# Latent adaLN sums in blocks of 128 rows by 1024 columns, with one sum tile, in a diffusion block on one Trainium2 core

## The chip, the cores and the metric

The kernel runs on one core of one Trainium2 chip. The metric is the device time of one execution in microseconds. Before the change the median of three runs is 1408.22 us (1406.82 to 1408.33). A profiled execution, from which all rows come, took 1407.89 us, of which the trace spans 1406.1 us from the first instruction to the last.

## What is computed

One layer of a diffusion backbone over 256 latent tokens x and 256 context tokens ctx, both 2048 wide, in fp32: neighbourhood attention with 16 heads, then a gated feed-forward part, each with a shift, a scale and a gate from a condition vector (adaLN). Cut to what matters:

```python
sh1, sc1, g1, sh2, sc2, g2 = adaln(cond_lat, w_ada, b_ada)   # silu(c) @ w_ada + b, six parts of 2048
h  = modulate(rms_norm(x, norm_mix_g), sh1, sc1)
hc = modulate(rms_norm(ctx, norm_mix_g), csh1, csc1)
y, _ = neighbourhood_attention(h, hc, w_qkv, q_g, k_g, rpb, w_o, False)
x  = x + g1 * y
hf = modulate(rms_norm(x, norm_ffn_g), sh2, sc2)
x  = x + g2 * conv_ffn(hf, w_up, conv_w, conv_b, w_down)
```

The change concerns the four parts g1, sc2, sh2 and g2 for the latent tokens: four products of one vector of 2048 with a matrix of 2048 x 2048.

## The kernel before

**Products.** All large products are made on TensorE (PE) in three parts: each weight tile of two blocks of 128 rows by up to 512 columns (a pair) is loaded by SP's queue into wr (four buffers), cast by ScalarE (ACT) into a high half wh (L166) and subtracted by VectorE (DVE) into a low half wl (L170). Two pairs are split ahead of use, and wl has two buffers, so pair n can be split when PE is done with pair n-2. PE then needs wh and wl. The stages: an opening with the norms and the first adaLN parts (to about 205 us); then, head group by head group, projections of q (two tiles of rows) and k and v (four tiles) over the 2048 columns of w_qkv, 512 columns at a time; the products with w_o; those with w_up; those with w_down.

**Attention** is cut into steps (scores, softmax, turn, weighted sum) that a list `side` hands out, some after every tile of a projection (`tick`). The turn transposes the softmax rows pr on PE into a bank ms, and ACT and DVE split the result into pth (L648) and ptl (L649). The weighted sum (L658, L661, L662) needs both, and its result is split by ACT (L578) and DVE (L579) into om, which the w_o products read. Heads 0 to 11 are done before the last v projection ends; their results wait in oT, and L579 also splits these. The last four heads run beside and behind the last v projection, up to the middle of the w_o products. The v tiles are split into vv (L572).

**The latent adaLN parts** are not products on PE. For one column group of 512 outputs, DVE multiplies each block of weight rows by the condition (one number per partition) and adds it into a tile acc (L289 for the first, L291 for the rest; 16 instructions for 2048 rows). Then PE transposes acc by four blocks of 128 into a bank ms (L299), and DVE reduces this (L302), adds the bias (L305) and, for the scale, the gain (L307). A second list `ada` hands these pieces out: a piece is a load of 512 KB into wa and two sums. Twelve column groups (g1, the scale gs2, the shift sh2) run between 220 and 665 us, with ADA_RATE pieces per tile of a projection (0.5 at four tiles, 0.1 at two) and 0.6 per pair in the w_o products; what is left is drained before the last w_o group. Four more, for g2, run in the w_up stage with two buffers. The loads run three pieces ahead. acc has two buffers, and a group's end (transposes, reduction) is called with the second piece of the next.

**What sets the order.** The program is written in the order in which the pieces are called, and a scheduler then puts each engine's instructions in one fixed row from its own estimate of durations, by priority and by when operands and buffers are free. Each engine works its row off in order; an instruction that waits holds all behind it. The banks ms (two buffers) serve adaLN transposes, scores, turns and weighted sums.

Of the kernel before, what the change touches and what calls it, by code (L numbers as in the profile page):

```python
# [9 lines left out]
F32 = mybir.dt.float32  # L10
F32R = mybir.dt.float32r
AF = mybir.ActivationFunctionType
ALU = mybir.AluOpType
AX = mybir.AxisListType

P = 128
D = 2048
T = 256
KD = D // P
# [6 lines left out]
CH = 512  # L26
KT = 2

RATE, RATE3 = 0.46, 0.36

ADA_RATE = {2: 0.1, 4: 0.5}

WA = 4

# [5 lines left out]
S_C, S_GM, S_GF, S_B, S_QG, S_KG = 0, 32, 48, 64, 160, 161  # L40
# [15 lines left out]
def block_kernel(  # L56
# [13 lines left out]
    nc = tc.nc  # L70
    cp = ctx.enter_context(tc.tile_pool(name="cp", bufs=1))
    wp = ctx.enter_context(tc.tile_pool(name="wp", bufs=1))
# [7 lines left out]
    def ms():  # L80
        return ps.tile([P, CH], F32, tag="ms", name="ms", bufs=2)
# [12 lines left out]
    sm = cp.tile([P, S_END], F32, name="sm")  # L94
    nc.sync.dma_start(sm, small)
    ident = cp.tile([P, P], F32, name="ident")
# [8 lines left out]
    for half in range(2):  # L105
# [3 lines left out]
            out=lo, in_=lo, pattern=[[1, GRID - WIN]], compare_op=ALU.is_ge, fill=NEG,  # L109
# [4 lines left out]
            out=hi, in_=hi, pattern=[[-1, GRID - WIN]], compare_op=ALU.is_ge, fill=NEG,  # L114
            base=WIN // 2 - 1 - WIN, channel_multiplier=1,
        )
    sT = cp.tile([P, KD, 2], F32, name="sT")
# [9 lines left out]
    g1T = cp.tile([P, KD], F32, name="g1T")  # L127
    sh2T = cp.tile([P, KD], F32, name="sh2T")
    gs2T = cp.tile([P, KD], F32, name="gs2T")
    g2T = cp.tile([P, KD], F32, name="g2T")  # L130
# [4 lines left out]
    nc.scalar.dma_start(rp, rpb)  # L135


    def wload(src, k0, kn, c0, cn, pool=None, bufs=WA):

        if pool:  # L140
            w = pool.tile([P, KT, CH], F32, tag="wa", name="wa", bufs=bufs)
        else:
            w = wp.tile([P, KT, CH], F32, tag="wr", name="wr", bufs=4)
        nc.sync.dma_start(
            w[:, :kn, :cn],
            src[k0 * P : (k0 + kn) * P, c0 : c0 + cn].rearrange("(k p) f -> p k f", p=P),
        )
        return w
# [122 lines left out]
    def ada_tasks(pool, i, c, dst, gcol=None, bufs=WA):  # L271

        st = {}

        def load(q):
            st[q] = wload(w_ada, q * KT, KT, i * D + c * CH, CH, pool, bufs)

        def part(q):
            w = st[q]
            if q == 0:
                st["acc"] = pool.tile([P, CH], F32, tag="acc", name="acc", bufs=2)
            acc = st["acc"]
            for k in range(KT):
                s = sT[:, q * KT + k, 0:1]
                if q == 0 and k == 0:
                    nc.vector.tensor_scalar_mul(acc, w[:, k, :], s)  # L289
                else:  # L290
                    nc.vector.scalar_tensor_tensor(  # L291
                        out=acc, in0=w[:, k, :], scalar=s, in1=acc, op0=ALU.mult, op1=ALU.add
                    )

        def finish():
            acc = st["acc"]
            sp = ms()
            for b in range(4):
                nc.tensor.transpose(sp[:, b * P : (b + 1) * P], acc[:, b * P : (b + 1) * P], ident)  # L299
            d = dst[:, 4 * c : 4 * c + 4]  # L300
            bc = S_B + i * KD + 4 * c
            nc.vector.tensor_reduce(  # L302
                out=d, in_=sp.rearrange("p (b t) -> p b t", t=P), axis=AX.X, op=ALU.add
            )
            nc.vector.tensor_add(d, d, sm[:, bc : bc + 4])  # L305
            if gcol is not None:
                nc.vector.scalar_tensor_tensor(  # L307
                    out=d, in0=d, scalar=1.0, in1=sm[:, gcol + 4 * c : gcol + 4 * c + 4],
                    op0=ALU.add, op1=ALU.mult,
                )  # L310

        return [(lambda q=q: load(q), lambda q=q: part(q)) for q in range(KD // KT)], finish

    def ada_pieces(cols, bufs=WA):

        loads = [l for pairs, _ in cols for l, _ in pairs]
        parts = [p for pairs, _ in cols for _, p in pairs]
        n = KD // KT

        def piece(i):  # L320
            if i == 0:
                for load in loads[: bufs - 1]:
                    load()
            if i + bufs - 1 < len(loads):
                loads[i + bufs - 1]()
            if i % n == 1 and i > n:
                cols[i // n - 1][1]()
            with tc.issue_after(last[0]), tc.issue_after(last[1]):
                if i < len(parts):
                    parts[i]()  # L330
                else:
                    cols[-1][1]()

        return [lambda i=i: piece(i) for i in range(len(parts) + 1)]


    hp = ctx.enter_context(tc.tile_pool(name="hp", bufs=1))
# [68 lines left out]
    loads = []  # L406
# [116 lines left out]
    ap = actx.enter_context(tc.tile_pool(name="ap", bufs=1))  # L523
# [154 lines left out]
            return [seq, w[0] + s[2] + t[2] + w[1] + s[3] + w[2] + t[3] + w[3]]  # L678
        return [seq + w[0] + s[2] + w[1] + t[2] + s[3] + w[2] + t[3] + w[3]]

    cols = [ada_tasks(ap, 2, c, g1T) for c in range(4)]
    cols += [ada_tasks(ap, 4, c, gs2T, S_GF) for c in range(4)]
    cols += [ada_tasks(ap, 3, c, sh2T) for c in range(4)]
    ada.extend(ada_pieces(cols))

    v, v1 = [[split_v([vsums[g][:, tt, :] for tt in range(4)], g)] for g in range(2)]
# [10 lines left out]
    k = split_k(out_of_psum(kps, kw))  # L697
    q = split_q(out_of_psum(project(0, 2), qw))
    for g in range(3):
        side.extend(sum(attention(g, q, k, v), []))  # L700
        c0 = (g + 1) * CH
# [238 lines left out]
        side.tick(1.6)  # L940
        ada.tick(0.25)

    later = ada_pieces([ada_tasks(fp, 5, c, g2T, bufs=2) for c in range(4)], 2)
    hfv = lambda kt, c: hf[:, kt, c]
    xgv = lambda kt, c: xg(kt, int(c.start > 0))
    for c0 in range(0, FF, CH):
# [82 lines left out]
```

## Time and profile before

| | |
|---|---|
| median of three runs | 1408.22 us (1406.82 to 1408.33) |
| profiled execution | 1407.89 us, span 1406.1 us |
| PE busy | 1380.3 us, 98% |
| DVE busy | 1028.0 us, 73% |
| ACT busy | 703.0 us, 50% |
| DMA moved | 317 MB, mean 226 GB/s |
| mean granted TensorE clock | 0.999 |

Busy time of PE is near to the whole span. Where PE is idle for a moment, the views name what it waited for: a tile, the engine and the line that wrote it last. A time such as 573.99 is counted from the first instruction of the span. Two instructions of an engine may overlap by a tenth of a microsecond in the rows, so what one costs its engine is read from start to start.

### The profile page before, as it was taken

To read this page: it belongs to the slowest core of one execution; us is meant where nothing else is said; L and a number is where in the kernel's file an instruction comes from. 1 tells how busy PE (TensorE), PEld (TensorE's weight loads), DVE (VectorE), ACT (ScalarE), POOL (GpSimd) and SP (SyncE) were. 2 spreads that over 40 slices of the span, in tenths; PEclk is the share of its full clock that TensorE was granted. 3 is DMA by queue.
4 is the path that set the end of the run, shared out by engine and by line. 5 is a ranking of instruction groups with operands and counts; after the bars stand their busy time and mean duration, and the time that the engine had idled before them with its cause. 6 is when DMAs were issued, how large, how long until landed. Compare 5 with 4: busy or idle time off the path is not lost.

```text
span 1406.1 us, 20819 instructions
## 1 busy us (share of the span) xinstructions
PE 1380.3 (98%) x7672; PEld 1167.7 (83%) x7672; DVE 1028.0 (73%) x1694; ACT 703.0 (50%) x1218; POOL 57.1 (4%) x57
## 2 busy tenths in 40 slices
PE   4999999999999999999999999999999999999999
PEld 2565778888888888888988888888888888888888
DVE  4555678879877979789898887878878675545454
ACT  4322254564444573554676565656556564333333
POOL 1000010121010121000000000000000000000000
PEclk9999999999999999999999999999999999999999
DMA  9998737767775868666767777777776666566554
GB/s 306 357 352 285 234 98 236 230 216 253 228 245 184 278 204 281 193 206 208 239 187 251 241 227 233 233 239 236 241 233 204 179 189 208 184 207 203 171 178 145
DMA packets 208919, 317.14 MB, mean 226 GB/s; under 512 B 23360, under 2 KB 87744, under 8 KB 208816
## 3 DMA queue, kind: packets, MB, share of 16 engines
q1 hardware_dynamic: 208688, 315.79, 71.7%
q8 instruction: 60, 0.98, 0.3%
q14 instruction: 43, 0.35, 0.1%
q10 hardware_dynamic: 128, 0.01, 0.0%
HBM read 312.75 MB, written 3.01 MB: 225 GB/s over the span
## 4 chain that ended last, share of the span: by engine, by line
PE 95%; DVE 2%; DMA 1%; SPq 1%; ACT 0%; issue 0%; DVEq 0%; ACTq 0%
PE pj L745 20%; PE pj L752 11%; PE mx L745 9%; PE pj L390 8%; PE pj L389 8%; PE pj L391 8%; PE ms L745 8%; PE mx L752 5%; PE ms L752 4%; PE mx L389 2%; PE ms L424 2%; PE mx L390 2%; PE mx L391 2%; PE ms L644 1%; SPq L418 1%; DMA xc<-in_ctxT 1%
## 5 line engine op out<-in xcount | busy, mean ns | idle before, releaser
L170 DVE TENSOR_TENSOR wl<-wr,wh 128x1024 fp32r<-128x1024 f32 (+2 forms) x425 | 478.6, 1127 | 253.1 <-ACT wh L166 127.2
L166 ACT CAST wh<-wr 128x1024 fp32r<-128x1024 f32 (+2 forms) x425 | 414.2, 976 | 485.2 <-PE pj L745 117.6
L390 PE MATMUL pj<-wl,hh 128*128 128x512 f32 x512 | 203.1, 397 | 0.0
L391 PE MATMUL pj<-wh,hl 128*128 128x512 f32 x512 | 200.0, 393 | 0.0
L389 PE MATMUL pj<-wh,hh 128*128 128x512 f32 x512 | 193.7, 397 | 2.5 <-ACT hh L463 2.5
L291 DVE SCALAR_TENSOR_TENSOR acc<-wa,sT,acc 128x512 f32<-128x512 f32 x240 | 185.0, 773 | 1.9
L745 PE MATMUL pj<-hf,wh 128*128 128x512 f32 x624 | 146.3, 391 | 0.0
L745 PEld LDWEIGHTS pj<-hf,wh 128*128 128x128 f32 x624 | 115.6, 188 | 23.0
L389 PEld LDWEIGHTS pj<-wh,hh 128*128 128x128 f32 x512 | 96.0, 189 | 26.6 <-issue 3.4
L390 PEld LDWEIGHTS pj<-wl,hh 128*128 128x128 f32 x512 | 96.8, 189 | 21.6 <-DVE wl L170 0.9
L391 PEld LDWEIGHTS pj<-wh,hl 128*128 128x128 f32 x512 | 96.5, 189 | 18.8
L745 PE MATMUL mx<-hf,wh 128*128 128x512 f32 x352 | 94.6, 390 | 0.0
L745 PE MATMUL ms<-hf,wh 128*128 128x512 f32 x336 | 90.5, 389 | 0.0
L752 PEld LDWEIGHTS pj<-hf,wl 128*128 128x128 f32 x624 | 77.5, 192 | 1.6
L752 PE MATMUL pj<-hf,wl 128*128 128x256 f32 x624 | 78.0, 283 | 0.0
L745 PEld LDWEIGHTS mx<-hf,wh 128*128 128x128 f32 x352 | 64.7, 188 | 12.3
L745 PEld LDWEIGHTS ms<-hf,wh 128*128 128x128 f32 x336 | 63.1, 188 | 13.3
L491 DVE TENSOR_TENSOR vsum<-vsum,mx 128x512 f32<-128x512 f32 x64 | 43.2, 684 | 34.2 <-PE mx L391 34.0
L897 ACT ACTIVATE y<-z,sm 128x256 f32<-128x256 f32 x86 | 51.8, 603 | 11.6 <-DVE z L880 10.0
L389 PE MATMUL mx<-wh,hh 128*128 128x512 f32 x128 | 52.7, 412 | 0.2
L424 PE MATMUL ms<-wx,s 128*32 128x512 f32 (+1 forms) x288 | 37.2, 587 | 15.4 <-DMA wx<-in_w_ada 15.4
L390 PE MATMUL mx<-wl,hh 128*128 128x512 f32 x128 | 50.7, 396 | 0.0
(264 smaller groups left out, 2036.8 us busy)
## 6 DMA issues: line engine op xcount, KB each, us to landing
wr<-in_w_up SPq DMA_DIRECT2D x160, 512.0 KB, 4.4
wa<-in_w_ada SPq DMA_DIRECT2D x128, 512.0 KB, 5.0
wr<-in_w_qkv SPq DMA_DIRECT2D x93, 512.0 KB, 4.2
wr<-in_w_down SPq DMA_DIRECT2D x63, 512.0 KB, 4.7
wx<-in_w_ada SPq DMA_DIRECT2D x56, 512.0 KB, 8.7
wr<-in_w_o SPq DMA_DIRECT2D x24, 512.0 KB, 5.0
wr<-in_w_down SPq DMA_DIRECT2D x45, 256.0 KB, 3.1
wr<-in_w_up SPq DMA_DIRECT2D x16, 384.0 KB, 3.8
```

Of the source, the lines that this page charges most:

```text
L166: a = nc.scalar.copy(hi[:, :kn, :cn], w[:, :kn, :cn])
L170: b = nc.vector.tensor_tensor(out=lo[:, :kn, :cn], in0=w[:, :kn, :cn], in1=hi[:, :kn, :cn].bitcast(F32), op=ALU.subtract,)
L291: nc.vector.scalar_tensor_tensor(out=acc, in0=w[:, k, :], scalar=s, in1=acc, op0=ALU.mult, op1=ALU.add)
L389: nc.tensor.matmul(pt, hh[:, kt, ts], wh[:, k, :], start=a, stop=False)
L390: nc.tensor.matmul(pt, hh[:, kt, ts], wl[:, k, :], start=False, stop=False)
L391: nc.tensor.matmul(pt, hl(kt, ts), wh[:, k, :], start=False, stop=z)
L418: load = nc.sync.dma_start(w.rearrange("p (k s f) -> p k s f", k=4, s=2)[:, :, which, :], w_ada[q * CH : (q + 1) * CH, c0 : c0 + n // 2].r ...
L424: nc.tensor.matmul(ap_[32 * k : 32 * k + 32, :n], s32[:, 4 * q + k, :], w[:, k * n : (k + 1) * n], start=(q == 0), stop=(q == 3), tile_pos ...
L491: nc.vector.tensor_add(acc[:, h0 + i, :], acc[:, h0 + i, :], pr_[i])
L745: nc.tensor.matmul(pts[b][:, : m.shape[-1]], wh[:, k, bs], m, start=(kt == 0 and t.start == 0), stop=False,)
L752: nc.tensor.matmul(pts[b][:, : m.shape[-1]], wl, m, start=False, stop=(kt == kn - 1))
L897: nc.scalar.activation(y, z, AF.Identity, bias=sm[:, S_CB + f : S_CB + f + 1], scale=sm[:, cw + 1 : cw + 2])
```

## The change

A block is now one block of 128 rows by 1024 columns, loaded as one tile of the same 512 KB and summed by one instruction. There are six column groups of 16 blocks in place of twelve of eight (and two in place of four for g2). acc is one tile of 1024 columns with one buffer. A group's end is a piece of its own behind the last block; it makes both halves in turn, each with four transposes into an own bank ms. A piece that ends a group loads nothing. With 6 x 17 = 102 pieces and ADA_RATE 0.6 in place of 0.5 at four tiles (five such projections of 32 tiles, four of two tiles with 16), the last piece is called with the last v projection, and none is left to the w_o products.

```diff
-ADA_RATE = {2: 0.1, 4: 0.5}
+ADA_RATE = {2: 0.1, 4: 0.6}
...
-        def load(q):
-            st[q] = wload(w_ada, q * KT, KT, i * D + c * CH, CH, pool, bufs)
-
-        def part(q):
-            w = st[q]
-            if q == 0:
-                st["acc"] = pool.tile([P, CH], F32, tag="acc", name="acc", bufs=2)
+        W = 2 * CH
+
+        def load(kt):
+            w = st[kt] = pool.tile([P, W], F32, tag="wa", name="wa", bufs=bufs)
+            c0 = i * D + c * W
+            nc.sync.dma_start(w, w_ada[kt * P : (kt + 1) * P, c0 : c0 + W])
+
+        def part(kt):
+            w, s = st.pop(kt), sT[:, kt, 0:1]
+            if kt == 0:
+                st["acc"] = pool.tile([P, W], F32, tag="acc", name="acc")
+                nc.vector.tensor_scalar_mul(st["acc"], w, s)
+                return
             acc = st["acc"]
-            for k in range(KT):
-                s = sT[:, q * KT + k, 0:1]
-                if q == 0 and k == 0:
-                    nc.vector.tensor_scalar_mul(acc, w[:, k, :], s)
-                else:
-                    nc.vector.scalar_tensor_tensor(
-                        out=acc, in0=w[:, k, :], scalar=s, in1=acc, op0=ALU.mult, op1=ALU.add
-                    )
+            nc.vector.scalar_tensor_tensor(
+                out=acc, in0=w, scalar=s, in1=acc, op0=ALU.mult, op1=ALU.add
+            )
...
+            for half in range(2):
+                sp = ms()
+                c4 = 8 * c + 4 * half
+                for b in range(4):
+                    nc.tensor.transpose(
+                        sp[:, b * P : (b + 1) * P], acc[:, (4 * half + b) * P :][:, :P], ident
+                    )
...
-            if i + bufs - 1 < len(loads):
-                loads[i + bufs - 1]()
-            if i % n == 1 and i > n:
-                cols[i // n - 1][1]()
+            if k < KD and loads:
+                loads.popleft()()
             with tc.issue_after(last[0]), tc.issue_after(last[1]):
-                if i < len(parts):
-                    parts[i]()
-                else:
-                    cols[-1][1]()
+                step()
...
-    cols = [ada_tasks(ap, 2, c, g1T) for c in range(4)]
+    cols = [ada_tasks(ap, 2, c, g1T) for c in range(2)]
```

Three places in the order of the instructions. Lines of the changed kernel have other numbers: L285 and L288 are the sums (L289 and L291 before), L298 the transposes (L299), L303 the reduction (L302), L167 the split into wl (L170), L575 the split of om (L579), L568 that of v (L572), L640 the turn (L644), L645 ptl (L649), L741 and L748 the products with w_o (L745, L752).

The first place is on DVE, in the last v projection, where the column groups of sh2T follow each other. Before:

```order
L636 RECIPROCAL rs<-rs 128x1 x2
L291 SCALAR_TENSOR_TENSOR acc<-wa,sT,acc 128x512 x3
L302 TENSOR_REDUCE sh2T<-ms 128x4
L649 TENSOR_TENSOR ptl<-ms,pth 128x4x128
L305 TENSOR_TENSOR sh2T<-sh2T,sm 128x4
L170 TENSOR_TENSOR wl<-wr,wh 128x1024
L289 TENSOR_SCALAR acc<-wa,sT 128x512
L291 SCALAR_TENSOR_TENSOR acc<-wa,sT,acc 128x512 x3
```

After, the whole stretch from the last sum of the fifth group (which stands more than 50 rows ahead) to the first sums of the sixth has no sum until the second reduction is done:

```order
L623 TENSOR_TENSOR ms<-ms,bt 128x256
L303 TENSOR_REDUCE sh2T<-ms 128x4
L628 TENSOR_REDUCE nm<-ms 128x1
L628 TENSOR_REDUCE nm<-mx 128x1
L306 TENSOR_TENSOR sh2T<-sh2T,sm 128x4
L632 RECIPROCAL rs<-rs 128x1 x2
L167 TENSOR_TENSOR wl<-wr,wh 128x1024
L303 TENSOR_REDUCE sh2T<-ms 128x4
L285 TENSOR_SCALAR acc<-wa,sT 128x1024
L306 TENSOR_TENSOR sh2T<-sh2T,sm 128x4
L645 TENSOR_TENSOR ptl<-ms,pth 128x4x128
L288 SCALAR_TENSOR_TENSOR acc<-wa,sT,acc 128x1024 x3
```

The sums of a group thus stand behind both reductions of the group before, where they stood beside them.

The second place is the start of the w_o products. On DVE (om the split heads, vv the split v tiles), before:

```order
L305 TENSOR_TENSOR sh2T<-sh2T,sm 128x4
L579 TENSOR_TENSOR om<-oT,om 128x256 x4
L170 TENSOR_TENSOR wl<-wr,wh 128x1024
L627 TENSOR_TENSOR ms<-ms,bt 128x256
L572 TENSOR_TENSOR vv<-pj,vv 128x512
L579 TENSOR_TENSOR om<-oT,om 128x256 x7
L632 TENSOR_REDUCE nm<-ms 128x1
L579 TENSOR_TENSOR om<-oT,om 128x256
L170 TENSOR_TENSOR wl<-wr,wh 128x1024 x2
```

and after:

```order
L575 TENSOR_TENSOR om<-oT,om 128x256 x4
L167 TENSOR_TENSOR wl<-wr,wh 128x1024
L568 TENSOR_TENSOR vv<-pj,vv 128x512
L575 TENSOR_TENSOR om<-oT,om 128x256 x2
L288 SCALAR_TENSOR_TENSOR acc<-wa,sT,acc 128x1024
L575 TENSOR_TENSOR om<-oT,om 128x256 x5
L645 TENSOR_TENSOR ptl<-ms,pth 128x4x128
L575 TENSOR_TENSOR om<-oT,om 128x256
L288 SCALAR_TENSOR_TENSOR acc<-wa,sT,acc 128x1024
L167 TENSOR_TENSOR wl<-wr,wh 128x1024 x2
```

Two wide sums now stand among the om splits, and four more follow, one behind each of the next wl. On PE the same place, before (the last steps of attention in front of and among the first w_o products):

```order
L623 MATMUL ms<-kh,qq 128x512
L624 MATMUL ms<-kl,qq 128x512
L625 MATMUL ms<-kh,qq 128x512
L662 MATMUL ms<-pth,vv 128x256
L745 MATMUL pj<-om,wh 128x512 x3
L658 MATMUL ms<-pth,vv 128x256
```

and after:

```order
L386 MATMUL pj<-wl,hh 128x512
L387 MATMUL pj<-wh,hl_111 128x512
L640 MATMUL ms<-ident,pr 128x128 x4
L741 MATMUL pj<-om,wh 128x512 x6
L748 MATMUL pj<-om,wl 128x256 x6
```

Six and six more products follow there with the next wh and wl, twice two and two with the fourth bank, and then eight with the third pair's wh and eight with its wl. The scores and weighted sums that stood in front before (eight more weighted sums ahead of the rows shown) come some 20 rows later, behind the products of nine pairs.

The third place is further on PE, between the second scores of head 14 and the turns of that head. Before:

```order
L625 MATMUL ms<-kh,qq 128x512
L752 MATMUL pj<-om,wl 128x256 x8
L745 MATMUL pj<-om,wh 128x512 x6
L644 MATMUL ms<-ident,pr 128x128 x4
L745 MATMUL pj<-om,wh 128x512 x2
```

and after:

```order
L621 MATMUL ms<-kh,qq 128x512
L741 MATMUL pj<-om,wh 128x512 x4
L748 MATMUL mx<-om,wl 128x256 x4
L741 MATMUL mx<-om,wh 128x512 x2
L640 MATMUL ms<-ident,pr 128x128 x8
L654 MATMUL ms<-pth,vv 128x256
```

Before, the second turn stood behind 22 further products; now both turns stand together, with ten products between them and the scores.

## Rows read from the trace of the kernel before

**Rows 1.** The page: busy time, share of the span and instructions of each engine.
```profile
PE 1380.3 (98%) x7672; PEld 1167.7 (83%) x7672; DVE 1028.0 (73%) x1694; ACT 703.0 (50%) x1218; POOL 57.1 (4%) x57
```

**Rows 2.** By stretch: length, busy PE, PEld, DVE, ACT, POOL, clock, DMA share, GB/s.
```profile
522.00:574.00 52.00, 52.00 (x258) 43.34 (x257) 47.87 (x82) 24.21 (x51) 5.57 (x5) 1.00 0.91 291
574.00:622.00 48.00, 46.49 (x278) 40.51 (x277) 34.99 (x64) 27.71 (x53) 0.00 (x0) 1.00 0.52 165
...
655.00:680.00 25.00, 22.71 (x161) 21.02 (x160) 19.65 (x40) 10.35 (x20) 0.00 (x0) 1.00 0.40 132
...
573.00:585.00 12.00, 11.98 (x69) 10.29 (x69) 11.94 (x26) 9.40 (x21) 0.00 (x0) 1.00 0.47 143
```

**Rows 3.** What PE waited for: us in total, times, longest.
```profile
PE ms L299 <- DVE acc L291: 1.0, 1, 1.0
PE pj L745 <- DVE om L579: 0.9, 1, 0.9
PE ms L752 <- DVE wl L170: 0.8, 1, 0.8
PE ms L661 <- DVE ptl L649: 0.6, 1, 0.6
```

**Rows 4.** DVE by line and shape: count, busy us, mean ns, idle before.
```profile
L170 DVE TENSOR_TENSOR wl<-wr,wh 128x1024 fp32r<-128x1024 f32 x340 | 416.3, 1225 | 200.6 <-ACT wh L166 95.4 <-issue 25.7 <-PE pj L752 23.1
...
L170 DVE TENSOR_TENSOR wl<-wr,wh 128x512 fp32r<-128x512 f32 x67 | 46.1, 691 | 46.2 <-ACT wh L166 27.1 <-PE pj L752 6.8 <-PE mx L390 3.8
```

**Rows 5.** DVE in order of time from wl 98 on: start, us, what.
```profile
555.07 1.22 DVE L170 TENSOR_TENSOR wl<-wr,wh 128x1024 fp32r<-128x1024 f32 x1
556.21 0.48 DVE L289 TENSOR_SCALAR acc<-wa,sT 128x512 f32<-128x512 f32 x1
556.72 2.33 DVE L291 SCALAR_TENSOR_TENSOR acc<-wa,sT,acc 128x512 f32<-128x512 f32 x3
...
569.01 1.51 DVE L291 SCALAR_TENSOR_TENSOR acc<-wa,sT,acc 128x512 f32<-128x512 f32 x1
...
574.16 0.74 DVE L291 SCALAR_TENSOR_TENSOR acc<-wa,sT,acc 128x512 f32<-128x512 f32 x1
574.82 0.68 DVE L572 TENSOR_TENSOR vv<-pj,vv 128x512 fp32r<-128x512 f32 x1
...
575.49 1.42 DVE L579 TENSOR_TENSOR om<-oT,om 128x256 fp32r<-128x256 f32 x4
...
582.18 2.36 DVE L170 TENSOR_TENSOR wl<-wr,wh 128x1024 fp32r<-128x1024 f32 x2
```

**Rows 6.** PE in order of time around the first w_o products.
```profile
573.99 0.28 PE L658 MATMUL ms<-pth,vv 128*128 128x256 f32 x1
...
575.96 0.96 PE L745 MATMUL pj<-om,wh 128*128 128x512 f32 x3
...
583.86 0.40 PE L752 MATMUL pj<-om,wl 128*128 128x256 f32 x2
```

**Rows 7.** The chain that ended last: what 32 and 16 products take.
```profile
712.29 1.91 PE mx L752 x16
...
727.23 7.28 PE pj L745 x32
```

**Rows 8.** One softmax (PE, ACT) and one turn, in order of time.
```profile
587.11 0.39 PE L625 MATMUL ms<-kh,qq 128*128 128x512 f32 x1
...
589.93 0.72 ACT L637 ACTIVATE pr<-pr,rs 128x512 f32<-128x512 f32 x1 [0.43 <-DVE rs L636]
...
608.74 0.60 PE L644 MATMUL ms<-ident,pr 128*128 128x128 f32 x4
...
609.99 0.69 DVE L649 TENSOR_TENSOR ptl<-ms,pth 128x512 fp32r<-128x512 f32 x1 [1.69 <-ACT pth L648]
```

**Rows 9.** The opening, columns as in rows 2.
```profile
30.00:35.00 5.00, 2.98 (x28) 0.88 (x27) 1.98 (x7) 0.11 (x1) 0.70 (x1) 0.91 1.12 328
35.00:40.00 5.00, 4.68 (x22) 3.25 (x22) 3.48 (x12) 2.45 (x6) 0.00 (x0) 0.75 1.09 345
```

## What the change does to the time: the prediction

> **What bounds the kernel now.** The first view is the page: PE is busy for 98% of the span and DVE for 73% [rows 1]. So a microsecond counts only where PE stands still, and an instruction taken from DVE is worth nothing unless PE was waiting for it. The second view is the busy time by stage [rows 2]. In the last v projection (522 to 574) PE is busy all of its 52.00 us. In the first products with w_o and the end of the attention (574 to 622) it stands still for 48 - 46.49 = 1.5 us, in the end of the w_o products (655 to 680) for 25 - 22.71 = 2.3 us. The third view names these waits [rows 3]: ptl 0.6 and om 0.9 in the first stretch; acc 1.0 and wl 0.8 in the second. The change can win 3.8 us here at most, 0.27% of the time, and it can lose wherever it puts an instruction between PE and what PE waits for. DVE is the engine to look at: in the last v projection it is busy for 47.87 of 52 us, and the start of the w_o products asks more of it.
>
> **The sums themselves.** Before, a block of 512 KB is two sums of 512 columns; now it is one of 1024, and there are as many blocks (128) and as many bytes. Three sums in a row take 2.33 us, so 0.78 each, and what follows a single one starts after 0.66 [rows 5]. The wide form is not in the trace. The next row is the subtraction L170, 691 ns at 512 columns and 1225 at 1024, so 0.53 us for 512 more [rows 4]: that makes 1.31 us for a wide sum in a chain and 1.2 for one alone. Below this stands 1.14 (a wide L170, start to start: 2.36 us for two), above it one narrow sum that took 1.51 [rows 5]. The first sum of a column, 0.48, becomes about 0.95 (0.75 if only its rate counts). DVE gains some 0.23 us per block, and where PE isn't waiting this is worth nothing. The transposes, reductions and bias sums are the same instructions in the same number. The loads keep their three pieces of lead; one is 128 lines of 4 KB in place of 256 of 2 KB, which I cost at nothing.
>
> **What the order shows: a pause, then a pile.** All six columns now write one tile acc, so a column's first sum waits for both groups of transposes of the column before, and these need both banks ms, which the attention uses too. At the fifth column PE has the two groups 24 products apart. On DVE this leaves no sum at all between the wl numbered 93 and 98 (I number the L170, one per pair of weight rows), where before there were four between every two; the sixth column's 16 sums come after number 98, with seven of them before 100 and the last six behind 101. So the column does not end with the last v projection but among the first w_o products, where before the DVE had next to no sums. The change takes ten blocks (20 narrow sums) out of the later w_o stage, and it puts six, with the end of a column, into the tightest place of the kernel.
>
> **First wait, om.** The first w_o product needs the split of head 0 (L579), which before was done 0.42 us after 575.49; PE came to it at 575.96 because 2 us of attention (three scores, twelve weighted sums) stood ahead [rows 5, 6]. Now these stand far behind, and PE comes to it straight from v and one group of transposes, at about 574.0 (v ends at 573.99 before; one group of transposes less inside, one more behind). DVE starts wl 98 at 555.07 as before, since PE frees its buffer then [rows 5]. From there to the split of head 0 the new order has three wl at 1.14 (3.4), eight instructions at 0.6 (two reductions, three ptl, three vv: 4.8), one add and two or three small ones (0.5), the first sum (0.95), three chained sums (3.9), six single ones (7.2) and 0.42: 21.2 us, so 576.3. PE waits 2.3 us. If the wide sums take 1.14 it is 1.6; if three of them are as slow as the slow one, 4.
>
> **Second wait, wl 102.** Before, number 102 was there at 583.4 and PE took it at 583.86, no slack [rows 5, 6]. Now, from the first om split: four om 1.33, wl 1.14, vv 0.6, eight om 2.67, ptl 0.6, two sums 2.4, wl 1.22, in all 10.0 us, so 585.9. PE after its first wait has 24 products of 512 columns at 0.2275 (7.28 us for 32) and 16 of 256 at 0.12 (1.91 for 16), 7.4 us [rows 7], so it stands at 583.7: 2.2 us of wait. Bounds 1.3 and 4. After that a pair costs PE 2.8 us and DVE one sum and one wl, 2.5, so DVE keeps up.
>
> **Third, the tail of the attention.** With its products spent early, PE has less to do between the steps of the last heads. Second scores of head 14 to the second group of their transposes: softmax takes 3.5 us (587.11 to 589.93 + 0.72 [rows 8]), PE has 0.23 + 0.91 + 0.48 + 0.46 + 0.4 = 2.5 in between: 1.1 of wait. The scores of head 15 need the bank of the weighted sum before: 0.3. The last turn: DVE now has two wl (2.3 us) ahead of the second ptl; from the first transposes, ptl starts after 1.25 [rows 8], so the second is done after 1.25 + 0.6 + 2.3 + 0.7 = 4.9, and PE is there after 2.8: 2.1 of wait, 0.6 before. The wait for om of head 15 (0.9) stays. Together 4.4 us against the 1.5 of before: 2.9 more. Bounds 0 and 5.5.
>
> **What goes.** The wait of the transposes for acc, the late wl behind it and what follows them [rows 3] have no cause any more, since no sums are left there: 2.3 us, next late is nothing that the trace shows. At least 0.6 of it. In the middle of the kernel the other five column changes are cost at nothing: PE comes to their transposes a pair or more after the last sum, and before, PE waited for acc and for wl once each, both times in the w_o stage [rows 3]; up to 2 us if a projection of two tiles, where the lead is less, meets the pile.
>
> **The sum**, on the profiled execution (1407.89 us, its span 1406.1; the median of three runs is 0.3 above): +2.3 + 2.2 + 2.9 - 2.3 = +5.1, that is **1413.0 us**. By the low bounds +0.6, by the high ones about +13.
>
> **The rivals.** (a) *Faster: nothing new waits.* If DVE has the splits ready in time, all 3.8 us of the two stretches go: 1404.1. For it: DVE is idle for 13 of 48 us between 574 and 622 [rows 2], room for all six late sums. Against it: where PE needs the splits, between 573 and 585, DVE is busy for 11.94 of 12 us [rows 2]. The Trainium skill, "VectorE: DVE Perf Modes", section on the TRN2 errata, says that an SBUF operation pays a fixed part per instruction, so that one large tile is cheaper than two; by that rule alone the 96 latent blocks free some 22 us of DVE and the change should be faster. The saving agrees with the 0.23 us from rows 4 and 5, but it falls where PE is not waiting. (b) *No change.* The waits for om and wl are as computed, but the attention runs meanwhile on ACT and DVE, the tail loses nothing against before, and the gain of 2.3 stands against the 2.5 or so that are left: 1408 to 1410. (c) *The sums wait for their loads.* DMA is at 0.91 of its time in the last v projection already [rows 2]; the pile asks for twelve blocks (6.3 MB) and six weight pairs (3.1 MB) in 30 us, 313 GB/s, where the v projection moved 291 at that share. A wide sum that waits holds all of DVE behind it, 2 to 4 us more: 1416.5. (d) *The clock.* Between 30 and 35 us PE had 2.98 busy of 5 us, and in the next 5 us the mean granted clock was 0.75, half of it at 1.2 GHz in place of 2.4 [rows 9]: some 1.2 us lost. Two waits of over 2 us could do the same: 1415 to 1416. The page "TensorE: Matmul & The Clock Gate" of the Trainium skill, Part 1, says that an idle array falls to half its clock; rows 9 agree, and whether waits as short as these do it no row shows. (e) *The change does not do what it says*: that is no case of its own here, as the order shows that the sixth column ends behind the last v projection, and the sum rests on it.
>
> **How the numbers follow.** The sum as worked out 0.45, (a) 0.10, (b) 0.25, (c) 0.13, (d) 0.07. A measurement can tell about 0.2%, 2.8 us, from no change: faster means under 1405.4, slower over 1411.0. Of the first case nearly all is slower, as are (c) and (d): 0.61; (b) and the low edge of the first case give 0.28 for the same, (a) 0.11 for faster. The range leaves out most of (a) and what lies beyond (c): 1406 to 1418; the first case alone spans 1410 to 1416.
>
> **What would show it.** In the trace after: no acc instruction on DVE between about 525 and 556; PE waits for om at about 574 and for wl at 583 to 586, 2 us each; wl waits of PE in the w_o end gone; waits for ptl and pr near the end of the attention longer than 1 us. Wrong would be a PE without gaps between 570 and 600, or waits at other column changes, above all in the q projections at 285, 420 and 500 us.

## The result, and the profile after

| | before | after |
|---|---|---|
| median, us | 1408.08 (six runs, 1406.82 to 1409.43) | 1413.03 (six runs, 1411.91 to 1414.87) |
| profiled execution, us | 1407.89, span 1406.1 | 1414.87, span 1413.1 |
| DVE busy, us | 1028.0 | 1005.3 |
| PE busy, us | 1380.3 | 1385.4 |

The ratio is 1.0037 (95% interval 1.0024 to 1.005): the changed kernel is slower by 4.9 us, with 22.7 us less work on DVE. The busy time of PE grew by 5.1 us with the same 7672 instructions, so part of the loss isn't idle time but slower products. The profiled execution is the slowest of the six, with a mean granted clock of 0.996; in the others it is 0.996 to 0.999, so the lower clock that is read below need not be in each of them.

In the changed kernel line numbers are lower by 3 or 4: L288 is the sum, L285 a column's first sum, L298 the transposes of the sum tile, L575 the split of om, L167 that of wl, L645 ptl, L741 and L748 the products with w_o. The same view as in [rows 2], by stretch of the changed kernel: length, busy PE, PEld, DVE, ACT, POOL, clock, DMA share, GB/s.

```profile
522.00:574.00 52.00, 52.00 (x255) 43.19 (x254) 39.27 (x66) 24.42 (x56) 6.51 (x6) 1.00 0.67 215
574.00:622.00 48.00, 43.46 (x250) 37.16 (x249) 37.82 (x62) 25.06 (x49) 0.24 (x1) 0.96 0.53 170
622.00:655.00 33.00, 31.31 (x179) 26.90 (x178) 26.70 (x46) 18.26 (x31) 0.00 (x0) 1.00 0.60 192
655.00:680.00 25.00, 24.94 (x161) 22.64 (x160) 16.74 (x31) 12.75 (x23) 0.00 (x0) 1.00 0.34 110
```

In the last v projection DVE has 8.6 us less to do than in [rows 2], which is worth nothing, as PE was full there. In the next stretch PE is idle for 4.5 us in place of 1.5 and its clock falls to 0.96. From 622 to 655, where before it was busy for all 33 us, it is idle for 1.7 us: the end of the attention now reaches into this stretch. The end of the w_o products is full: 2.2 us won.

What PE waited for, as in [rows 3]:

```profile
PE pj L741 <- DVE om L575: 3.1, 2, 2.6
PE ms L640 <- ACT pr L633: 1.3, 1, 1.3
PE ms L657 <- DVE ptl L645: 1.2, 1, 1.2
PE pj L741 <- ACT wh L163: 0.6, 1, 0.6
PE mx L748 <- DVE wl L167: 0.3, 1, 0.3
PE pj L748 <- DVE wl L167: 0.3, 1, 0.3
```

DVE from wl 98 on, beside [rows 5]. The line ahead of it is the last sum of the fifth column:

```profile
524.76 1.27 DVE L288 SCALAR_TENSOR_TENSOR acc<-wa,sT,acc 128x1024 f32<-128x1024 f32 x1
...
556.02 1.22 DVE L167 TENSOR_TENSOR wl<-wr,wh 128x1024 fp32r<-128x1024 f32 x1 [1.84 <-PE pj L386]
...
557.76 0.74 DVE L285 TENSOR_SCALAR acc<-wa,sT 128x1024 f32<-128x1024 f32 x1
...
559.10 4.55 DVE L288 SCALAR_TENSOR_TENSOR acc<-wa,sT,acc 128x1024 f32<-128x1024 f32 x3
561.73 1.92 DVE L288 SCALAR_TENSOR_TENSOR acc<-wa,sT,acc 128x1024 f32<-128x1024 f32 x1
...
573.41 1.91 DVE L288 SCALAR_TENSOR_TENSOR acc<-wa,sT,acc 128x1024 f32<-128x1024 f32 x1
...
576.44 1.27 DVE L288 SCALAR_TENSOR_TENSOR acc<-wa,sT,acc 128x1024 f32<-128x1024 f32 x1
577.64 1.42 DVE L575 TENSOR_TENSOR om<-oT,om 128x256 fp32r<-128x256 f32 x4
...
586.39 2.35 DVE L167 TENSOR_TENSOR wl<-wr,wh 128x1024 fp32r<-128x1024 f32 x2
```

The row at 561.73 is the third of the three at 559.10, shown by itself. No sum stands between 526 and 557.8, then sixteen, with the last ones among the splits. PE at the same place, beside [rows 6], and in the end of the attention:

```profile
574.69 0.39 PE L387 MATMUL pj<-wh,hl 128*128 128x512 f32 x1
574.92 0.60 PE L640 MATMUL ms<-ident,pr 128*128 128x128 f32 x4
578.11 2.24 PE L741 MATMUL pj<-om,wh 128*128 128x512 f32 x6 [2.59 <-DVE om L575]
580.15 1.48 PE L748 MATMUL pj<-om,wl 128*128 128x256 f32 x6
...
587.65 1.22 PE L748 MATMUL pj<-om,wl 128*128 128x256 f32 x8 [0.30 <-DVE wl L167]
...
612.46 0.66 PE L640 MATMUL ms<-ident,pr 128*128 128x128 f32 x4 [1.30 <-ACT pr L633]
...
624.88 0.38 PE L657 MATMUL ms<-ptl,vv 128*128 128x256 f32 x1 [1.23 <-DVE ptl L645]
```

The last product of v comes, PE takes one group of transposes, and then stands 2.59 us for the split of head 0. The six products behind it take 2.04 us from start to start, and six at full clock take 1.46 (e11, below). The clock is the last number but two in these stretches of 4 us:

```profile
574.00:578.00 4.00, 1.51 (x9) 1.06 (x7) 4.00 (x6) 3.46 (x11) 0.24 (x1) 1.00 1.04 399
578.00:582.00 4.00, 3.90 (x14) 3.33 (x15) 4.00 (x9) 2.58 (x6) 0.00 (x0) 0.62 0.65 213
582.00:586.00 4.00, 4.00 (x23) 3.46 (x22) 4.00 (x9) 1.38 (x2) 0.00 (x0) 0.95 0.77 241
```

A mean of 0.62 means that most of the 4 us after the wait ran at 1.2 GHz in place of 2.4. The two stretches behind the wait lose 4 x 0.38 + 4 x 0.05 = 1.7 us of PE by it.

### The profile page after: what moved, and what is told of

Same layout as the page of the kernel before. It is cut to its first block, busy times and chain, and to the rows that moved or that the text cites. A ratio compares the mean times of both kernels' runs of the same rounds, so it can differ in the third digit from the quotient of the medians.

```text
span 1413.1 us, 20704 instructions
## 1 busy us (share of the span) xinstructions
PE 1385.4 (98%) x7672; PEld 1169.7 (83%) x7672; DVE 1005.3 (71%) x1566; ACT 702.7 (50%) x1218; POOL 55.7 (4%) x57
## 4 chain that ended last, share of the span: by engine, by line
PE 95%; DVE 2%; SPq 1%; DMA 1%; ACT 1%; issue 0%; POOL 0%; DVEq 0%; ACTq 0%
PE pj L741 20%; PE pj L748 11%; PE mx L741 9%; PE pj L386 8%; PE pj L385 8%; PE pj L387 8%; PE ms L741 7%; PE mx L748 5%; PE ms L748 4%; PE mx L385 2%; PE ms L420 2%; PE mx L386 2%; PE mx L387 2%; PE ms L640 1%; SPq L414 1%; DVE wl L167 1%
## 5 line engine op out<-in xcount | busy, mean ns | idle before, releaser
L167 DVE TENSOR_TENSOR wl<-wr,wh 128x1024 fp32r<-128x1024 f32 (+2 forms) x425 | 477.6, 1125 | 259.2 <-ACT wh L163 134.8
L288 DVE SCALAR_TENSOR_TENSOR acc<-wa,sT,acc 128x1024 f32<-128x1024 f32 x120 | 155.1, 1293 | 2.3 <-DMA wa<-in_w_ada 1.8
L741 PE MATMUL pj<-hf,wh 128*128 128x512 f32 x624 | 145.8, 390 | 0.0
L741 PEld LDWEIGHTS pj<-hf,wh 128*128 128x128 f32 x624 | 115.7, 188 | 23.1
L386 PEld LDWEIGHTS pj<-wl,hh 128*128 128x128 f32 x512 | 96.8, 189 | 21.2 <-DVE wl L167 0.9
L741 PE MATMUL mx<-hf,wh 128*128 128x512 f32 x352 | 94.6, 390 | 0.0
L741 PE MATMUL ms<-hf,wh 128*128 128x512 f32 x336 | 90.5, 389 | 0.0
L748 PEld LDWEIGHTS pj<-hf,wl 128*128 128x128 f32 x624 | 77.5, 192 | 1.6
L748 PE MATMUL pj<-hf,wl 128*128 128x256 f32 x624 | 78.0, 283 | 0.0
L741 PEld LDWEIGHTS mx<-hf,wh 128*128 128x128 f32 x352 | 64.7, 188 | 12.3
L741 PEld LDWEIGHTS ms<-hf,wh 128*128 128x128 f32 x336 | 63.1, 188 | 13.3
```

The source lines that it names most:

```text
L167: b = nc.vector.tensor_tensor(out=lo[:, :kn, :cn], in0=w[:, :kn, :cn], in1=hi[:, :kn, :cn].bitcast(F32), op=ALU.subtract,)
L288: nc.vector.scalar_tensor_tensor(out=acc, in0=w, scalar=s, in1=acc, op0=ALU.mult, op1=ALU.add)
L386: nc.tensor.matmul(pt, hh[:, kt, ts], wl[:, k, :], start=False, stop=False)
L741: nc.tensor.matmul(pts[b][:, : m.shape[-1]], wh[:, k, bs], m, start=(kt == 0 and t.start == 0), stop=False,)
L748: nc.tensor.matmul(pts[b][:, : m.shape[-1]], wl, m, start=False, stop=(kt == kn - 1))
```

## The experiments

The theory that stood behind the prediction is called A: the one sum tile holds up each column, and the sums of the last column pile up where the first w_o products wait for DVE. The rivals tried are B (wide sums and wide blocks cost by themselves), C (sums wait for loads) and D (the denser handing out costs). In later expectations A' is the same theory said of the place alone: what costs is where the last column's sums stand. Each run was compared with the kernel before on the same chip, median 1407.7 to 1407.9. The whole picture first, in medians:

| sums | sum tiles | load tiles | rate 0.5 | 0.6 | 0.65 | 0.7 |
|---|---|---|---|---|---|---|
| narrow | 2 | as before | 1407.8 (before) | 1405.4 (e4) | 1406.1 (e10) | 1410.7 (e8) |
| narrow | 1 | as before | | 1420.4 (e6) | | |
| wide | 1 | 4 | 1418.4 (e9) | 1413.0 (after) | 1406.3 (e5) | |
| wide | 1 | 3 | | 1416.1 (e2) | | |
| wide | 2 | 3 | | 1412.7 (e1) | 1408.7 (e7) | |
| narrow in a wide tile | 1 | 4 | | 1415.3 (e3) | | |

### e1 and e2: two sum tiles, with three load tiles

```diff
-WA = 4
+WA = 3
...
-                st["acc"] = pool.tile([P, W], F32, tag="acc", name="acc")
+                st["acc"] = pool.tile([P, W], F32, tag="acc", name="acc", bufs=2 if bufs > 2 else 1)
```

e2 has the first of the two edits only.

> The changed kernel with two sum tiles in place of one; to make room for the second, three load tiles in place of four (e2 has that alone). Theory A (the one sum tile makes each column wait for the transposes of the one before, and the sums that pile up behind that wait stand among the first w_o products): in the order the sums stand two or three between every two wl again and none behind wl 100, from wl 98 to the first split of om are 17.3 us in place of 21.3, so om is ready at about 573 and wl 102 at about 580, before PE wants them; both waits go, the end of the w_o products keeps its gain of 2.3, the end of the attention may still lose up to 2.9: 1406 to 1409, some 5 us under e2. Theory B (wide sums, or lines of 4 KB, are what costs, whatever the order): as the changed kernel, 1412 to 1414.

> The changed kernel with three load tiles in place of four, one sum tile: the counterpart of e1. The order on DVE is that of the changed kernel but for one or two sums. Theories A and B: 1411.5 to 1413.5, the wait for om 1 to 2 us, the one for wl 1 to 2. If the sums waited for their loads (theory C), three tiles would make it worse: over 1415.

Measured: e1 1412.65 us (ratio 1.0044, 1.003 to 1.0057), e2 1416.12 (1.0058, 1.0045 to 1.007). The second tile wins 3.5 us, not 5, and e1 is no better than the changed kernel: by its number alone it falls where B had it. In e1 the pile is gone from the order, as theory A had it, but DVE and PE show the next thing that was late:

```profile
560.41 1.29 DVE L288 SCALAR_TENSOR_TENSOR acc<-wa,sT,acc 128x1024 f32<-128x1024 f32 x1 [3.15 <-DMA wa<-in_w_ada]
```
```profile
577.44 2.93 PE L741 MATMUL pj<-om,wh 128*128 128x512 f32 x6 [3.89 <-DVE om L575]
```

A sum waited 3.15 us for its block, all of DVE behind it. The splits of om began at 576.30, the first took 1.08 us in place of 0.42, and om came 4.4 us after the 573 expected. So C is a real cost with three load tiles: sums waited 8.5 us for loads in e1 and 14.2 in e2, against 1.8 in the changed kernel with four. In e2 this also made PE wait 1.5 us for wl around 420 and 506. So e1 against e2, both with sums that wait for loads, doesn't measure the tile cleanly. No run has two wide sum tiles beside four load tiles, and what the tile alone costs in the wide form stays open.

### e3: the same pile with narrow sums

```diff
+            for h in (slice(0, CH), slice(CH, W)):
...
-                out=acc, in0=w, scalar=s, in1=acc, op0=ALU.mult, op1=ALU.add
...
+                    out=acc[:, h], in0=w[:, h], scalar=s, in1=acc[:, h], op0=ALU.mult, op1=ALU.add
```

The first sum of a column is cut in two in the same way.

> The changed kernel, but each sum of 1024 columns as two of 512 in the two halves of the same tile; loads, the one sum tile and the rate as changed. Theory A: the pile stays, each of its blocks takes 0.25 us more, so wl 102 is 0.7 later: 1413 to 1415. Theory B, with the wide sum as the cost (one instruction of 1.3 us that holds the splits behind it): 1408 to 1410.

Measured: 1415.29 us (1.0053, 1.0041 to 1.0066). PE waits 1.98 us for om and 0.55 for wl, at the same two products. B falls for the width of the sums: with narrow sums in the same tile and the same order on PE the loss is there, and 2.3 us larger in the medians (0.3 us over the range of A). Where these 2.3 us come from is not shown: the two waits are shorter together than in the changed kernel (2.5 us against 2.9), and the two profiled executions differ by 0.4 us. The wide blocks are still in e3; e5 settles them.

### e4: the rate alone

```diff
-ADA_RATE = {2: 0.1, 4: 0.5}
+ADA_RATE = {2: 0.1, 4: 0.6}
```

This is an edit of the kernel before.

> The kernel before with the rate of 0.6 in place of 0.5 alone: narrow sums, two sum tiles. In the order the last sum stands before wl 99, so nothing is left for the w_o products. Theory A: the boundary stays without waits (12.9 us from wl 98 to the first split of om), the wait for acc and the wl behind it at the end of the w_o products go: 1408.1 - 2.3 = 1405.8, between 1404.5 and 1407.5. Theory D (the denser handing out fills DVE in the v projections and is what costs): 1411 or more.

Measured: 1405.37 us (0.9983, 0.9974 to 0.9991), the best version that was run and under both kernels. D falls at this rate. The waits of PE outside the opening, and the end of the w_o products:

```profile
PE pj L745 <- DVE om L579: 0.5, 1, 0.5
PE ms L661 <- DVE ptl L649: 0.2, 1, 0.2
```
```profile
655.00:680.00 25.00, 24.94 (x186) 23.74 (x184) 16.22 (x31) 13.21 (x24) 0.00 (x0) 1.00 0.49 162
```

PE is busy for 24.94 us of these 25, as in the changed kernel. What the change wins there comes from the rate, not from the width.

### e5: the changed kernel, a little faster handed out

```diff
-ADA_RATE = {2: 0.1, 4: 0.6}
+ADA_RATE = {2: 0.1, 4: 0.65}
```

> The changed kernel with the rate of 0.65 in place of 0.6 alone: wide sums, one sum tile, four load tiles. In the order the last sum now stands before wl 98, so that 8.6 us of DVE lie between wl 98 and the first split of om in place of 21.3. Theory A' (what costs is the place of the last column's sums, between wl 98 and the first w_o products, whatever the width and the number of sum tiles): om is ready some 10 us before PE, the waits for om and for wl at 575 to 588 go and with them the lower clock; the end of the w_o products keeps its gain of 2.3. If the end of the attention still loses 2.2 as in the changed kernel, 1408.0, if not, 1405.8: 1405.5 to 1408.5. Theory B (the wide sums and blocks themselves): 1412 or more.

Measured: 1406.34 us (0.9989, 0.998 to 0.9998). One number moves the changed kernel by 6.7 us, from slower than before to a little faster, with the same tile, the same width, the same loads.

```profile
574.00:622.00 48.00, 46.96 (x287) 41.03 (x286) 32.01 (x62) 27.46 (x54) 0.00 (x0) 1.00 0.42 132
655.00:680.00 25.00, 24.79 (x176) 23.09 (x176) 15.26 (x29) 11.08 (x19) 0.00 (x0) 1.00 0.47 154
```

From 574 to 622 PE stands still for 1.0 us in place of 4.5, and the clock is 1.00. So neither the wide sums nor the wide blocks cost by themselves. One detail was expected wrongly: om wasn't ready 10 us ahead but at 575.8, since the last splits of v stand ahead of it on DVE and come only with the last v products. That is just in time.

### e6: one sum tile in the narrow form

```diff
-                st["acc"] = pool.tile([P, CH], F32, tag="acc", name="acc", bufs=2)
+                st["acc"] = pool.tile([P, CH], F32, tag="acc", name="acc", bufs=1)
```

An edit of e4, and the only one.

> e4 (narrow sums, rate 0.6) with one sum tile in place of two, and nothing else. In the order the last column's first sum moves from wl 95 to behind wl 100, two sums stand before the first split of om and the others between wl 101 and 108. Theory A (the shared tile delays the column): the delay is seen in the order, but with 11.9 us of DVE between wl 98 and the first split, om is in time; the end of the attention may lose up to 2.2 against e4: 1405.4 to 1408. If a shared tile costs wherever the sums stand, by waits for the transposes at each of the eleven column changes: 1411 or more.

Measured: 1420.41 us (1.0088, 1.0074 to 1.0102), 15.0 us over e4: far over the range of A, and in the open range of the second line. The longest waits of PE that e4 doesn't have:

```profile
PE pj L752 <- DVE wl L170: 2.1, 1, 2.1
PE ms L661 <- DVE ptl L649: 2.0, 1, 2.0
PE ms L644 <- ACT pr L637: 1.4, 1, 1.4
PE ms L545 <- DVE qn L539: 0.9, 1, 0.9
```

and what DVE stood still for:

```profile
DVE acc L289 <- PE ms L299: 6.4, 5, 1.9
```

The first sums of the columns wait for the transposes on DVE, 6.4 us in five of them, and everything on DVE waits behind them. One of these is at 446, where the q projection then waits (qn, 0.9 us, and 1.2 us for kh and kl in the scores just ahead): a column change in the middle does cost when little stands ahead on PE. Counted from start to start (each product's time to the start of the next, less what its shape usually takes), the projections between 400 and 522 lose 2.9 us more than in e4, and the stretch from 574 to 650 loses 12.0 us more: at the boundary and in the end of the attention, with a mean clock of 0.94 from 574 to 627. That the shared tile costs is shown most plainly here, by one edit, for the narrow form.

### e7 and e8: how far the rate carries

e7 is e1 with 0.65 in place of 0.6, e8 the kernel before with 0.7 in place of 0.5.

> e1 (two sum tiles, three load tiles) with the rate of 0.65: the last sum stands before wl 98. e1 had a DVE that waited 3.15 us for a load at 557 us, which made om late by as much. Theory A' with that load as the cause in e1: no wait for om, 1405.5 to 1408.5. If e1 was late for another reason than the load (two wide sum tiles as such), 1411 to 1413.

> The kernel before with the rate of 0.7 in place of 0.5: the last sum stands before wl 94. Theory A': as e4, 1405.4, between 1404 and 1406.5, as nothing is left to win at the boundary. If the denser sums make PE wait in the projections before (wl at the two-tile ones, 420 and 500 us), 1407 or more.

Measured: e7 1408.74 us (1.0009, 1.0 to 1.0018), a little over the range, and e8 1410.68 (1.0013, 1.0004 to 1.0022), where its second line had it. In e7 the wait for om is 0.5 us, which speaks against two wide tiles as such. That the load was the cause in e1 is read from its trace and not tested apart, as the new rate moved the sums too. What is left in e7 is a wait of 2.0 us for ptl at the end of the attention, with the clock at 0.59 behind it. No sum starts there between 552 and 680 us, so this wait needs no late sum; e11 comes back to it. In e8 PE waits 3.0 us in a q projection, behind a row of seven sums, and not at the boundary:

```profile
450.31 0.63 PE L545 MATMUL mx<-ident,qn 128*128 128x128 f32 x4 [3.02 <-DVE qn L539]
```

The pile can be moved, and where it lands in a two-tile projection PE waits as long (3.02 us) as for om in the changed kernel (2.59). The median of e8 is 2.5 us over its profiled execution (1408.2), so this wait is not all of it. The profiled execution has a mean clock of 0.999. In six of the eleven it is 0.994 to 0.996, and these take 1409.6 to 1412.3 us, so a fall of the clock that the trace doesn't hold is a likely part of the rest; where it falls, no run shows.

### e9: the changed kernel at the old rate

```diff
-ADA_RATE = {2: 0.1, 4: 0.6}
+ADA_RATE = {2: 0.1, 4: 0.5}
```

> The changed kernel with the rate of 0.5, that of the kernel before: wide sums, one tile. In the order the sixth column now begins behind wl 101 and ends behind wl 133, and 13.7 us of DVE stand between wl 98 and the first split of om in place of 21.3. Theory A': om is ready at 569, 5 us before PE, no wait at the boundary; the sums are back at the end of the w_o products, so some of the 2.3 us of before may be back there: 1406 to 1410, under the changed kernel though the sums end later. A theory by which the time grows with how late the sums end: over 1413.

Measured: 1418.37 us (1.0071, 1.0059 to 1.0083). PE is busy for all of 574 to 590, as expected, though om came only at about 575.2, and the total is far off. It falls where the last theory had it (over 1413). The loss stands at the other end of the w_o products, PE first and then two stretches around and behind the wait:

```profile
675.19 1.94 PE L298 MATMUL ms<-ident,acc 128*128 128x128 f32 x8 [8.80 <-DVE acc L288]
```
```profile
668.00:676.00 8.00, 0.81 (x4) 0.84 (x5) 7.80 (x14) 3.16 (x8) 0.00 (x0) 0.70 0.10 34
676.00:680.00 4.00, 3.95 (x19) 3.58 (x18) 2.15 (x6) 0.20 (x1) 0.00 (x0) 0.50 0.02 4
```

The last column begins at 582, its sums run to the end of the w_o products, and what comes next needs the column: 8.8 us of wait in place of the 1.0 before [rows 3]. The one tile and the pieces that now only end a column can both make it late, and e9 doesn't separate them. Before the change the last sum of this stage started at 665.4 us, here at 673.8. At 0.6 the same column collides with the beginning of the stage, at 0.65 with neither.

### e10: between e4 and e8

The kernel before with the rate of 0.65.

> The kernel before with the rate of 0.65: the last sum stands before wl 97. Between e4 (0.6, 1405.4) and e8 (0.7, which waited 3.0 us at 447 us behind seven sums in a row in a q projection). Here no more than four sums stand in a row at that place (wl 77). Theory A': 1404.5 to 1406, as e4. If the density of the sums in the projections costs by itself, 1407 to 1410.

Measured: 1406.06 us (0.9989, 0.998 to 0.9997), twelve runs from 1403.81 to 1411.59, the widest spread of all. PE waits nowhere over 0.5 us outside the opening in the profiled execution, the fastest one. The median lies at the upper edge of what was expected for A' (1404.5 to 1406), and its difference from e4 is within that spread.

### e11: the last six sums left out

```diff
+            if i == 3 and c == 1 and kt >= 10:
+                return
             acc = st["acc"]
```

> The changed kernel with the last six sums of the sixth column left out (their loads stay; part of the shift of the second norm is then missing from the output): those that stand behind the first splits of om. The order on DVE is unchanged up to there, 21.3 us from wl 98. Theory: the wait for om (2.2) stays and with it the lower clock, the wait for wl 102 goes as it is ready 1.8 us sooner, and the end of the attention waits as before the change (1.8 us in all in place of 4.0): 1409.5 to 1411.5. If the end of the attention waits because its products were spent early on PE and not because of the late sums: 1412 or more.

Measured: 1406.55 us (0.9991, 0.9982 to 0.9999), 3 us under the range. PE around the first w_o product, and two stretches:

```profile
576.29 0.63 PE L300 MATMUL ms<-ident,acc 128*128 128x128 f32 x4 [1.70 <-DVE acc L290]
576.67 1.62 PE L743 MATMUL pj<-om,wh 128*128 128x512 f32 x6
```
```profile
574.00:578.00 4.00, 2.30 (x15) 1.88 (x14) 4.00 (x8) 4.00 (x13) 0.65 (x1) 1.00 0.97 331
578.00:582.00 4.00, 4.00 (x26) 3.57 (x25) 4.00 (x10) 2.04 (x4) 0.00 (x0) 1.00 1.02 380
```

The wait at the boundary stays, now in two halves (the transposes wait for the last sum, om is there when they are done). It is 1.7 us and the clock stays at 1.00: 1.7 us saved that were expected to stay. And the end of the attention, counted from start to start as in e6, stands still for 0.9 us between 600 and 650, where the changed kernel stands for 5.1 and the kernel before for 2.3.

This doesn't tell the two theories of the tail apart, since leaving out the sums also changed the order on PE. In the changed kernel 108 products with w_o run without a break from 578.11 on, and the next weighted sums come at 603.09. In e11 it is 40 products, with weighted sums at 584.54. So in e11 the w_o products are not spent early either. The last two splits of ptl show what differs. The changed kernel, e7 and e11:

```profile
621.88 2.35 DVE L167 TENSOR_TENSOR wl<-wr,wh 128x1024 fp32r<-128x1024 f32 x2
624.14 0.68 DVE L645 TENSOR_TENSOR ptl<-ms,pth 128x512 fp32r<-128x512 f32 x1
```
```profile
614.79 2.36 DVE L167 TENSOR_TENSOR wl<-wr,wh 128x1024 fp32r<-128x1024 f32 x2 [0.51 <-ACT wh L163]
617.07 0.69 DVE L645 TENSOR_TENSOR ptl<-ms,pth 128x512 fp32r<-128x512 f32 x1
617.80 0.57 PE L657 MATMUL ms<-ptl,vv 128*128 128x256 f32 x1 [2.03 <-DVE ptl L645]
```
```profile
614.90 1.37 DVE L647 TENSOR_TENSOR ptl<-ms,pth 128x512 fp32r<-128x512 f32 x2 [0.33 <-ACT pth L646]
616.37 2.36 DVE L167 TENSOR_TENSOR wl<-wr,wh 128x1024 fp32r<-128x1024 f32 x2
```

In the first two, two wl stand ahead of the last ptl, and PE waits 1.23 and 2.03 us for it. In e11 both ptl stand ahead of the two wl, and PE doesn't wait for them. In e7 no sum starts between 552 and 680 us, and between 600 and 650 it loses 5.0 us, a lower clock included. So the longer tail goes with the order on PE and DVE and doesn't need late sums. What the late sums add to it in the changed kernel is not shown.

## Why the prediction was right, step by step

The total, 1413.0 us, fell together with the median of 1413.03, and the mechanism is the one that was predicted. Not every term had its size, and that the two agree to a tenth is luck: the sum was made for the profiled execution, which grew by 7.0 us and not by 5.1.

- **Pause, then pile.** Right. No sum between 526 and 557.8 (predicted 525 to 556), then sixteen.
- **The sums.** A wide sum alone takes 1.20 us from start to start, as predicted from the other form. Behind one another they start 1.31 us apart, as predicted too; three in a row take 4.47, where 3.9 was predicted, since the third is a slow one (1.92 us at 561.73). A first sum takes 0.66, where 0.95 was predicted.
- **First wait, om.** Predicted 2.3 us, measured 2.59. From wl 98 to the end of the first split it is 22.0 us, against 21.2: two slow sums (1.92 us at 561.73 and 1.91 at 573.41) gave 0.6 each, smaller rows went the other way. The prediction had allowed for slow sums in its upper bound.
- **Second wait, wl 102.** Predicted 2.2, measured 0.30, and the number was there when it was predicted, 9.5 us after the first w_o product began. It was PE that came later, on a clock of 0.62: from the first w_o product to the eight ahead of wl 102 it took 7.25 us (578.11 to 585.36), in e11 at full clock 5.67. Wait, clock and second wait are 2.59 + 1.6 + 0.30 = 4.5 us together, which is 2.3 + 2.2.
- **Rival (d), the clock.** It came true in its mechanism and not in its price: the slow products used up time in which PE would have waited for wl 102 anyway. The prediction added the clock on top of both waits. The page "TensorE: Matmul & The Clock Gate" of the Trainium skill, Part 1, says that an idle array falls to half its clock; the waits of 1.98 (e3), 2.59 and 3.89 us (e1) at this place agree, the one of 3.02 in e8 does not (below).
- **The tail.** Predicted 4.4 us in place of 1.5. The four waits are 1.30 (pr, predicted 1.1), 0.35 (wl; 0.3 was predicted, for a bank), 1.23 (ptl, predicted 2.1) and 0.46 (om of head 15, predicted 0.9), 3.3 in all. Against the 1.5 of before these waits are 1.8 more, where 2.9 was predicted, so ptl and om were sized too large. From start to start, small gaps included, the stretch from 600 to 650 loses 2.8 against before, so the agreement with 2.9 is in part luck. The reason that was given, w_o products spent early and two wl ahead of the last ptl, is what the trace shows, and e7 waits for ptl in the same way without a late sum. e11 can't speak against it, as the order on PE is another there.
- **What goes.** Predicted 2.3, measured 2.2 (24.94 of 25 us, 22.71 before). That nothing is late next was nearly right: the first product of the next stage waits 0.6 us for wh, which is new. The text left open which part of the change wins this; e4 shows that it is the rate.
- **The middle columns.** Cost at nothing, and PE waits at none of them in the changed kernel. e6 shows that this isn't safe: in the narrow form the change at 446 us costs 2 us or more.
- **Rival (c), the loads.** Not in the changed kernel: the sums waited 1.8 us for loads in all, with four tiles. With three it is 8.5 to 14.2 (e1, e2).
- **Rivals (a) and (b).** DVE did win 22.7 us, 0.18 for each of the 128 blocks, where the prediction had 0.23 (its 22 us were for the 96 latent blocks ahead of g2). This is in the direction that "VectorE: DVE Perf Modes" of the Trainium skill gives in its section on the TRN2 errata (one large tile pays the fixed part once), and e5 is what comes of it without the pile: 1406.3, no faster than narrow sums at a good rate (e4).

Of the 7.0 us between the two profiled spans, 0.95 are there before all this: wl 98 starts at 556.02 in place of 555.07 [rows 5]. e11, which has the same order up to that place, starts it at 555.09, so this comes from the execution and not from the change. It fits the clock of the opening: over the first 100 us it is 0.97, with 82.8 us of busy PE, against 0.98 and 81.6 before and 0.98 and 81.5 in e11. Without it the profiled loss is 6, and the median loss is 4.9.

## What to carry to other kernels

Work that is handed out beside a full engine costs by where its last pieces land: find the place where the full engine waits for the same helper next, and see to it that the pieces end before it, since 0.05 in one rate was worth 6.7 us here (e5), and the wide sums, with 22.7 us of saved helper time, 2.3 at most (e3). Look at the order on every engine after each such edit, too, because the scheduler may move more than the edit did (e11). Giving up the second buffer of an accumulator ties each group's start to the readout of the one before, and the last group comes late (in the narrow form 15.0 us by one edit). When two waits stand close together, a cost between them (here the clock) is paid out of the second, so the prices of neighbouring terms are not to be added blindly.

## What the runs showed of the chip that was not expected

- The granted clock doesn't follow from the length of a wait alone. After 1.70 us (e11) it stayed at 1.00, after 1.98 (e3) and 2.59 (after) it fell to 0.67 and 0.62 in the 4 us behind, and after 3.02 us in a q projection (e8) it stayed at 1.00:

```profile
450.00:454.00 4.00, 3.69 (x20) 3.13 (x21) 1.51 (x3) 0.69 (x1) 0.00 (x0) 1.00 0.74 267
```

  What differs between these places is not settled. Each is one execution: that of e8 has a mean clock of 0.999, and its ten others have 0.994 to 0.999.
- A wide sum takes 1.20 us from start to start when another instruction follows and 1.31 when a sum on the same tile does; in the narrow form it is 0.66 and 0.78 [rows 5].
- A few instructions of DVE are slow: most wide sums last 1.27 us, those at 561.73 and 573.41 last 1.92 and 1.91. In e11 the same three sums take 4.55 us again. What makes them slow is not settled.
